# Product-key queries of a two-layer kernel: 16 column groups for both token blocks in split fp32r, against one block of 128 tokens at a time in fp32

## The chip, the cores and the metric

The kernel runs on one core of a Trainium2 chip. The metric is the device time of one execution in microseconds (us). The kernel before took 1683.35 us (median of three runs, 1680.67 to 1683.51).

## The reference

Two transformer layers on 256 tokens of width 1024. The part that changes is the first layer's feed-forward, a product-key mixture of 16384 experts, cut here to what matters:

```python
def peer_ffn(h, w_query, sub_keys, expert_u, expert_v):     # h: 256 x 1024, in two blocks of 128 tokens
    def block(xt):
        q = (xt @ w_query).reshape(128, 8, 2, 128)           # w_query: 1024 x 2048
        s = jnp.einsum('thpd,hpnd->thpn', q, sub_keys)       # 128 scores for each of 8 heads x 2 halves
        s_top, i_top = lax.top_k(s, 16)
        cand = ...                                           # 16 x 16 sums of the two halves
        best, pos = lax.top_k(cand, 16)
        idx, g = ..., jax.nn.softmax(best, axis=-1)          # 16 experts for each token and head
        act = jax.nn.gelu(jnp.einsum('td,thkd->thk', xt, expert_u[idx]))
        return jnp.einsum('thk,thkd->td', g * act, expert_v[idx])
```

Every token so gathers 128 expert rows of 8 KB (u and v side by side, `uv`). The second layer needs a vector `mod2` from its own matrix `w_ada_2`, which depends on no token.

## The kernel before

The program is one stream of instructions for each engine, laid out by a scheduler from the order and the priorities of the Python code; each engine then runs its own stream in order and waits on semaphores. SP's stream issues all plain loads, POOL's stream the gathers.

Most of the on-chip memory is one tile, `arena`, of eight slots of 2 MB (a slot is four units of 1024 columns). Slots 0 to 3 take weights in turn; slots 4 to 7 hold, in this part of the program, scratch for queries (`qT`), keys, scores (`S`) and the top-16 lists.

`_peer_scores` (line 638) makes the queries and scores. `_modulate` writes the normed tokens as two halves, `hh` and `hl` in fp32r (hi and lo, features on partitions), and the weight is split in the same way (`_halves`, line 258: ACT rounds, line 262; DVE subtracts, line 263). A product is then three fp32r matmuls, lines 274 to 276, with the weight stationary and all 256 tokens moving. There are 16 groups of 128 query columns, four to a load of `w_query` (line 716, into slots 0, 3, 1, 2); line 738 makes the scores of a load's four groups for both token blocks, against the keys. `todo[tb]` collects generators of DVE work: `top16` (lines 697 to 712) for each load and block, later `route` (lines 772 to 798), which turns the lists into `idx` (experts of a token block, transposed by PE at line 790) and `gT`. `fill(budget, blocks)` emits some of it: 2 us of block 0's after each weight group, all that is left of block 0 in one go in `_peer_experts`, and block 1's in portions of 4.5 us inside the expert loop.

`_peer_experts` first transposes the tokens to rows for the experts (`by_tokens`, line 812: `ht`, hi and lo) and forms `mod2`'s first two thirds: eight loads of `w_ada_2` (2 MB each, line 823) go through slots 0, 3, 1, 2 twice, each consumed by eight small fp32 matmuls (line 207; 32 for a set of four loads). Then comes the expert loop, over two blocks of 32 rounds r of four tokens each. For each token POOL issues a gather of 128 rows, 1 MB (line 840), into a ring of ten buffers: units 0, 2 (slot 0), 4, 6 (slot 1), 30, 22, 24 of the arena and three `uv` tiles. PE spreads the token over partitions (line 857), DVE multiplies and sums (line 859), and after four tokens PE adds the weighted v rows to `acc` (line 866), which frees the four buffers.

After the loop `_front2` and `_moe` compute the second layer.

Of the kernel before, what the change touches and what calls it, by code (L numbers as in the profile page):

```python
# [9 lines left out]
F32 = mybir.dt.float32  # L10
F32R = mybir.dt.float32r
# [3 lines left out]
AF = mybir.ActivationFunctionType  # L15
ALU = mybir.AluOpType
# [3 lines left out]
P = 128  # L20
T = 256
D = 1024
# [15 lines left out]
def _layout(i):  # L38
# [32 lines left out]
    def tiled(w, n):  # L71
        k, m = w.shape
        return w.reshape(k // P, P, m // n, n).transpose(2, 1, 0, 3).reshape(m // n, P, (k // P) * n)
# [9 lines left out]
    a["w_o_attn"] = tiled(f["w_o_attn"][0], 1024)[0]  # L83
    a["w_o_lru"] = tiled(f["w_o_lru"][0], 512)
    a["w_out"] = tiled(f["w_out"][0], 512)
    a["w_query"] = tiled(f["w_query"][0], P).reshape(4, 4, P, D).transpose(0, 2, 1, 3).reshape(4, P, 4 * D)
    a["keysT"] = f["sub_keys"][0].reshape(16, P, P).transpose(2, 0, 1).reshape(P, 16 * P)
    a["uv"] = np.concatenate([f["expert_u"][0], f["expert_v"][0]], axis=1)
    a["w_in_2"] = tiled(f["w_in_2"][0], 512)
# [149 lines left out]
def _modulate(nc, k, gain, mod, s_shift, s_scale, sq, tmp, hi, lo, y=None):  # L239

    A = tmp[:, 3 * T:3 * T + NC]
    nc.vector.scalar_tensor_tensor(A, mod[:, 8 * s_scale:8 * s_scale + 8], 1.0, gain, ALU.add, ALU.mult)
    if y is None:
        y = _stats(nc, k, sq, tmp)
    for c in range(NC):
        sh = mod[:, 8 * s_shift + c:8 * s_shift + c + 1]
        nc.vector.scalar_tensor_tensor(sq[:, c, :], k.xT[:, c, :], A[:, c:c + 1], y, ALU.mult, ALU.mult)
        nc.scalar.activation(hi[:, c, :], sq[:, c, :], AF.Identity, bias=sh)
        nc.vector.scalar_tensor_tensor(lo[:, c, :], sq[:, c, :], sh, hi[:, c, :].bitcast(F32), ALU.add, ALU.subtract)
# [386 lines left out]
def _peer_scores(tc, nc, ap, k, stage):  # L636

    ps = k.ps
    k.pe = stage.enter_context(tc.tile_pool(name="pe1", bufs=1, side="right"))
    off = [0]  # L640

    def scratch(shape, dt=F32):
        n = int(np.prod(shape))
        v = k.arena[:, 64 * T + off[0]:64 * T + off[0] + n]
        off[0] += n
        assert off[0] <= 64 * T
        if dt != F32:
            v = v.bitcast(dt)
        if len(shape) == 2:
            v = v.rearrange("p (a b) -> p a b", b=shape[1])  # L650
        if len(shape) == 3:
            v = v.rearrange("p (a b c) -> p a b c", b=shape[1], c=shape[2])
        return v

    k.scratch, k.off = scratch, off
    hh, hl = k.hr[:, :8, :], k.hr[:, 8:, :]
    off[0] = 4 * T
    _modulate(nc, k, k.col("norm2_g"), k.mod, 3, 4, scratch([NC, T]), k.arena[:, 64 * T:68 * T], hi=hh, lo=hl)

    def lin(raw, out):  # L660

        _cols3(tc, nc, k.wide, raw.rearrange("p (c n) -> p c n", c=NC), hh, hl, [out])
        k.fill(2.0, (0,))

    k.todo = todo = [[], []]

    def fill(budget, blocks=(0, 1)):

        for tb in blocks:
            while todo[tb] and budget > 0:  # L670
                got = next(todo[tb][0], None)
                if got is None:
                    todo[tb].pop(0)
                else:
                    tc.keep_in_program_order(got[0])
                    budget -= got[1]

    k.fill = fill


    off[0] = 4 * D
    qT = scratch([16, T])
    keys = scratch([16, P])
    k.S = S = [scratch([16, P]) for _ in range(2)]
    nc.sync.dma_start(keys.rearrange("p a n -> p (a n)"), ap["keysT"])
    k.best1 = best1 = []
    for tb in range(2):
        off[0] = tb * 3 * D
        best1.append((scratch([8, 2, 16]), scratch([8, 2, 16], U32), [scratch([T]) for _ in range(2)],
                      scratch([8, 16]), scratch([8, 16], U32), off[0]))  # L690

    def top16(tb, p):

        sc, (m, ix, s2, best, pos, _) = S[tb], best1[tb]
        for n in range(4 * p, 4 * p + 4):
            mv, iv, rest = m[:, n // 2, n % 2, :], ix[:, n // 2, n % 2, :], s2[n % 2][:, :P]
            yield nc.vector.max(mv[:, :8], sc[:, n, :]), 0.3
            yield nc.vector.max_index(iv[:, :8], mv[:, :8], sc[:, n, :]), 0.3
            yield nc.vector.match_replace(rest, mv[:, :8], sc[:, n, :], -3.0e38), 0.3
            yield nc.vector.max(mv[:, 8:], rest), 0.3  # L700
            yield nc.vector.max_index(iv[:, 8:], mv[:, 8:], rest), 0.3
        hs = slice(2 * p, 2 * p + 2)
        cand = sc[:, 4 * p:4 * p + 4, :].rearrange("p n k -> p (n k)").rearrange("p (h a b) -> p h a b", a=16, b=16)
        yield nc.vector.tensor_tensor(cand, m[:, hs, 0, :, None].to_broadcast([P, 2, 16, 16]),
                                      m[:, hs, 1, None, :].to_broadcast([P, 2, 16, 16]), ALU.add), 0.7
        for h in (2 * p, 2 * p + 1):
            ch, c2 = cand[:, h - 2 * p].rearrange("p a b -> p (a b)"), s2[h % 2]
            yield nc.vector.max(best[:, h, :8], ch), 0.43
            yield nc.vector.max_index(pos[:, h, :8], best[:, h, :8], ch), 0.45
            yield nc.vector.match_replace(c2, best[:, h, :8], ch, -3.0e38), 0.43  # L710
            yield nc.vector.max(best[:, h, 8:], c2), 0.43
            yield nc.vector.max_index(pos[:, h, 8:], best[:, h, 8:], c2), 0.45

    for p, sl in enumerate((0, 3, 1, 2)):
        raw = k.slot(sl)
        nc.sync.dma_start(raw, ap["w_query"][p])
        bq = [ps.tile([P, 512], F32, name="ps", tag="ps") for _ in range(2)]
        for q in range(2):
            b = bq[q]
            if p + q == 0:  # L720

                w = [_halves(tc, nc, k.wide, raw[:, u * D:(u + 1) * D].rearrange("p (c n) -> p c n", c=NC)) for u in range(3)]
                for c in range(NC):
                    for u, (wh, wl) in enumerate(w):
                        o = bq[u // 2][:, u % 2 * T:(u % 2 + 1) * T]
                        nc.tensor.matmul(o, wh[:, c], hh[:, c, :], start=c == 0 and u != 1, stop=False)
                        nc.tensor.matmul(o, wh[:, c], hl[:, c, :], start=False, stop=False)
                        nc.tensor.matmul(o, wl[:, c], hh[:, c, :], start=False, stop=c == NC - 1 and u != 0)
            for j in range(2):
                u = 2 * q + j  # L730
                if p or u == 3:
                    lin(raw[:, u * D:(u + 1) * D], b[:, j * T:(j + 1) * T])
            nc.scalar.copy(qT[:, 4 * p + 2 * q:4 * p + 2 * q + 2, :].rearrange("p a t -> p (a t)"), b)
        for tb in range(2):
            b = ps.tile([P, 512], F32, name="ps", tag="ps")
            for j in range(4):
                n = 4 * p + j
                nc.tensor.matmul(b[:, j * P:(j + 1) * P], qT[:, n, tb * P:(tb + 1) * P], keys[:, n, :],
                                 start=True, stop=True)
            nc.scalar.copy(S[tb][:, 4 * p:4 * p + 4, :].rearrange("p a n -> p (a n)"), b)  # L740
            todo[tb].append(top16(tb, p))


GU = 3
# [2 lines left out]
def _peer_experts(tc, nc, ap, k):  # L747

    with (
# [3 lines left out]
        tc.tile_pool(name="psum_a", bufs=2, space=PSUM) as k.pa,  # L753
    ):
        one, scratch, off, todo, S, best1 = k.pe, k.scratch, k.off, k.todo, k.S, k.best1
        hr = k.hr
        identr = one.tile([P, P], F32R, name="identr")
        nc.vector.tensor_copy(identr, k.ident)
        iota16 = one.tile([P, 16], F16, name="iota16")
# [44 lines left out]
        ht = one.tile([P, 2, 2, D], F32R, name="ht")  # L804

        def by_tokens(tb):
            for a in range(2):
                for g in range(2):
                    b = k.pa.tile([P, 512], F32, name="pa", tag="pa")
                    for j in range(4):  # L810
                        src = hr[:, 8 * a + 4 * g + j, tb * P:(tb + 1) * P].bitcast(F32)
                        nc.tensor.transpose(b[:, j * P:(j + 1) * P], src, k.ident)  # L812
                    nc.scalar.copy(ht[:, tb, a, 512 * g:512 * g + 512], b)


        k.csr2 = _silu_cols(nc, k, k.persist2, "c_2", "csr2")
# [6 lines left out]
                nc.sync.dma_start(ahead[g], ap[name][g])  # L823
            return ahead[g]

        by_tokens(0)
        sums = [pb.tile([P, D], F32, name="bc", tag="bc")[:, :512] for _ in range(2)]
        _ada_load(nc, load, k.csr2, sums[0], 0, range(4), "w_ada_2")
        k.fill(1e9, (0,))
        by_tokens(1)  # L830
        _ada_set(nc, k, one, sums[0], 0, k.mod2, "b_ada_2")
        _ada_load(nc, load, k.csr2, sums[1], 1, range(4), "w_ada_2")
# [54 lines left out]
def _front2(tc, nc, ap, k):  # L887
# [8 lines left out]
    with (  # L896
# [8 lines left out]
        room = k.extra.tile([P, 4 * D], F32, name="room", tag="ring")  # L905
        causal = room[:, 3584:3712]
        nc.sync.dma_start(causal, ap["masks"][:, P:2 * P])
        hh, hl = k.hr[:, :8, :], k.hr[:, 8:, :]
        sy = k.slot(1).rearrange("p (j t) -> p j t", t=T)
        big = k.slot(2).rearrange("p (j t) -> p j t", t=T)  # L910
# [444 lines left out]
```

## Time and profile before

| what | us |
|---|---|
| median of three runs | 1683.35 |
| the profiled execution | 1682.16 |
| its span, first to last instruction | 1680.3 |
| first gather issued | 348.94 |
| last gather landed | 1012.73 |

The page lists 1301.6 us of PE busy time (77% of the span), 855.5 us of DVE (51%), 308.9 us of ACT (18%). The page's slices are 42 us long: the program's first layer up to the scores lies in slices 1 to 7, the queries and the top-16 in slices 7 to 9, the expert loop in slices 9 to 25. The trace gives times from the first instruction on. A fp32 matmul shows as two records of PE, a fp32r matmul as one. Records of PE overlap, so the pitch is the distance of starts. In rows of the timeline `x3` means three instructions merged, and what stands in brackets at the end is idle time before the row and who ended it.

### The profile page before, as it was taken

The page shows a single profiled execution, that of the slowest core. Times are in us where ns is not written, and L with a number is a line of the kernel's source. Part 1 is how long each engine was busy: PE and PEld are TensorE (multiplying, and loading weights), DVE is VectorE, ACT ScalarE, POOL GpSimd, SP SyncE. Part 2 cuts the span into 40 slices and gives each one's busy share as a digit, 9 for nine tenths or more (in the row PEclk, how much of TensorE's full clock was granted, in tenths as well). Part 3 has the DMA queues.
Part 4 walks back from the last instruction along what each step waited for, and adds up shares of the span by engine and source line. Part 5 has one row for each costly group of instructions (what it writes and reads, how often), then busy time and mean ns, then how long its engine had stood idle before and what let it go on. Part 6 is the DMA issues. An engine that isn't in the chain of part 4 may idle for free.

```text
span 1680.3 us, 19564 instructions
## 1 busy us (share of the span) xinstructions
PE 1301.6 (77%) x7782; PEld 777.2 (46%) x7782; DVE 855.5 (51%) x1844; ACT 308.9 (18%) x545; POOL 242.1 (14%) x260
## 2 busy tenths in 40 slices
PE   5999999957776777777776777999978665665665
PEld 2878898623333333333333335899943221221211
DVE  4779677968884454554555446874442120121111
ACT  3567544210000000100000004443220000000000
POOL 0000000033333343333333320000000000000000
PEclk8999999978889998898889988999989888897888
DMA  9557762699999999999999997564579999999997
GB/s 377 209 224 277 278 249 101 238 371 419 420 421 420 420 420 420 415 420 420 420 420 420 420 410 277 185 250 151 225 312 429 425 427 427 427 426 429 425 429 298
DMA packets 64992, 594.56 MB, mean 354 GB/s; under 512 B 7008, under 2 KB 8064, under 8 KB 12672
## 3 DMA queue, kind: packets, MB, share of 16 engines
q1 hardware_dynamic: 28032, 324.80, 47.5%
q0 software_dynamic: 36864, 268.45, 38.6%
q8 instruction: 63, 1.03, 0.3%
q14 instruction: 33, 0.27, 0.0%
HBM read 592.15 MB, written 1.08 MB: 353 GB/s over the span
## 4 chain that ended last, share of the span: by engine, by line
DMA 43%; PE 37%; DVE 13%; issue 3%; ACT 2%; POOL 1%; SPq 0%; DVEq 0%; POOLq 0%; ACTq 0%
DMA arena<-w 19%; DMA arena<-uv,idx 12%; DMA uv<-uv,idx 9%; PE bc L857 4%; PE ps L274 4%; PE ps L276 4%; PE ps L275 4%; PE acc L866 4%; DVE arena L859 4%; DMA ring<-w 2%; PE ps L1208 2%; DVE uv L859 2%; PE ps L993 2%; PE pa L1141 1%; DVE wl L263 1%
## 5 line engine op out<-in xcount | busy, mean ns | idle before, releaser
L857 PE MATMUL bc<-ht,identr 128*128 128x512 f32 x1024 | 334.8, 455 | 172.9 <-DVE arena L859 114.6
L857 PEld LDWEIGHTS bc<-ht,identr 128*128 128x128 f32 x1024 | 191.1, 207 | 346.5 <-DVE arena L859 168.0
L859 DVE SCALAR_TENSOR_TENSOR arena<-arena,bc 128x1024 f32<-128x1024 f32 x181 | 219.9, 1219 | 170.0 <-PE bc L857 88.4
L840 POOL DMA_INDIRECT arena<-uv,idx x181 | 171.0, 945 | 660.8 <-PE pa L812 348.5
L274 PE MATMUL ps<-hr,wh 128*128 128x256 f32 x648 | 185.7, 287 | 0.0
L275 PE MATMUL ps<-hr,wh 128*128 128x256 f32 x648 | 184.5, 285 | 0.0
L276 PE MATMUL ps<-hr,wl 128*128 128x256 f32 x648 | 184.1, 284 | 0.4 <-DVE wl L263 0.4
L263 DVE TENSOR_TENSOR wl<-arena,wh 128x1024 fp32r<-128x1024 f32 (+1 forms) x116 | 139.6, 1214 | 80.1 <-ACT wh L262 79.6
L1208 PE MATMUL ps<-arena,xg 128*32 128x512 f32 x832 | 116.3, 688 | 56.1 <-DMA arena<-w 56.1
L866 PE MATMUL acc<-arena,wz 128*32 128x512 f32 x724 | 153.5, 736 | 6.5 <-DVE wz L862 6.5
L262 ACT CAST wh<-arena 128x1024 fp32r<-128x1024 f32 (+1 forms) x116 | 119.4, 1041 | 138.6 <-PE ps L275 98.7
L859 DVE SCALAR_TENSOR_TENSOR uv<-uv,bc 128x1024 f32<-128x1024 f32 x75 | 91.2, 1220 | 77.0 <-PE bc L857 45.0
L274 PEld LDWEIGHTS ps<-hr,wh 128*128 128x128 f32 x648 | 124.1, 192 | 5.1 <-issue 2.8
L860 ACT ACTIVATE s<-s 128x4 f32<-128x4 f32 x64 | 13.1, 205 | 615.1 <-DVE arena L859 366.4
L276 PEld LDWEIGHTS ps<-hr,wl 128*128 128x128 f32 x648 | 124.1, 192 | 1.4 <-DVE wl L263 1.1
L275 PEld LDWEIGHTS ps<-hr,wh 128*128 128x128 f32 x648 | 124.1, 192 | 0.9 <-issue 0.8
L1218 DVE TENSOR_TENSOR hid<-hid,ps 128x512 f32<-128x512 f32 x8 | 5.5, 688 | 209.1 <-PE ps L1208 209.1
L1231 PE MATMUL ps<-arena,hidT 128*32 128x512 f32 x400 | 65.5, 765 | 39.0 <-DMA arena<-w 36.0
L866 PE MATMUL acc<-uv,wz 128*32 128x512 f32 x300 | 90.8, 711 | 0.6 <-DVE wz L862 0.5
L1208 PEld LDWEIGHTS ps<-arena,xg 128*32 128x32 f32 x832 | 24.6, 117 | 130.1 <-DMA arena<-w 66.1
L840 POOL DMA_INDIRECT uv<-uv,idx x75 | 70.9, 945 | 87.8 <-PE acc L866 66.7
L866 PEld LDWEIGHTS acc<-arena,wz 128*32 128x32 f32 x724 | 29.1, 127 | 74.7 <-issue 44.8
(360 smaller groups left out, 1535.8 us busy)
## 6 DMA issues: line engine op xcount, KB each, us to landing
arena<-w SPq DMA_DIRECT2D x74, 2048.0 KB, 39.2
arena<-w_ada SPq DMA_DIRECT2D x24, 2048.0 KB, 10.5
arena<-w_in SPq DMA_DIRECT2D x18, 2048.0 KB, 9.0
ring<-w SPq DMA_DIRECT2D x18, 2048.0 KB, 39.2
arena<-w_query SPq DMA_DIRECT2D x4, 2048.0 KB, 11.1
arena<-w SPq DMA_DIRECT2D x6, 1024.0 KB, 15.3
arena<-w_o_lru SPq DMA_DIRECT2D x2, 2048.0 KB, 10.5
arena<-w_out SPq DMA_DIRECT2D x2, 2048.0 KB, 9.4
```

Source lines behind the costliest of these rows:

```text
L262: nc.scalar.copy(hi, w)
L263: nc.vector.tensor_tensor(lo, w, hi.bitcast(F32), ALU.subtract)
L274: nc.tensor.matmul(out, wh[:, c, cs], rh[:, c, :], start=c == 0, stop=False)
L275: nc.tensor.matmul(out, wh[:, c, cs], rl[:, c, :], start=False, stop=False)
L276: nc.tensor.matmul(out, wl[:, c, cs], rh[:, c, :], start=False, stop=c == kc - 1)
L840: nc.gpsimd.indirect_dma_start(out=uv, out_offset=None, in_=ap["uv"], in_offset=bass.IndirectOffsetOnAxis(ap=idx[:, t:t + 1], axis=0))
L857: nc.tensor.matmul(b[:, 512 * h:512 * h + 512], pick, ht[:, tb, a, 512 * h:512 * h + 512], start=a == 0, stop=a == 1)
L859: nc.vector.scalar_tensor_tensor(u, u, 1.0, b, ALU.mult, ALU.mult, accum_out=s4[:, j:j + 1])
L866: nc.tensor.matmul(acc[32 * j:32 * j + 32, 512 * h:512 * h + 512], w[:, j, 31 - r:63 - r], vs[j][:, 512 * h:512 * h + 512], start=r == 0, ...
L993: nc.tensor.matmul(b[:, j * T:(j + 1) * T], w[:, c, (2 * q + j) * P:(2 * q + j + 1) * P], src[:, c, :], start=c == 0, stop=c == 3)
L1208: nc.tensor.matmul(b[32 * j:32 * j + 32, :], xg[:, c, 32 * j:32 * j + 32], w[:, cc, j, :], start=c == 0, stop=c == NC - 1)
L1231: nc.tensor.matmul(y[h][32 * j:32 * j + 32, :], hidT[:, f, 32 * j:32 * j + 32], w[:, j], start=f == 0, stop=f == 3)
```

## The change

The queries are computed in fp32 without any split, one block of 128 tokens at a time. The 128 tokens are stationary (`hF`, features on partitions), and a load of `w_query`, now 512 columns of all 1024 rows, is moving. The queries come out with tokens on partitions, so that PE transposes them (line 740) ahead of the scores (line 746). Block 0's four loads are done first, then block 1's with the same four loads, which stay in their slots until then. `hF` takes the place of `hr`. `by_tokens` now makes the hi and lo halves itself, from `hF`, and its first call stands behind the rest of block 0's routing.

```diff
-    a["w_query"] = tiled(f["w_query"][0], P).reshape(4, 4, P, D).transpose(0, 2, 1, 3).reshape(4, P, 4 * D)
+    a["w_query"] = tiled(f["w_query"][0], 512)
...
-    hh, hl = k.hr[:, :8, :], k.hr[:, 8:, :]
+    k.hF = hF = k.persist.tile([P, NC, T], F32, name="hF", tag="hr")
...
+    for tb in range(2):
+        ts = slice(tb * P, (tb + 1) * P)
+        for c in range(NC):
+            nc.vector.scalar_tensor_tensor(sq[:, c, ts], k.xT[:, c, ts], A[:, c:c + 1], y[:, ts], ALU.mult, ALU.mult)
+            nc.scalar.activation(hF[:, c, ts], sq[:, c, ts], AF.Identity, bias=k.mod[:, 24 + c:25 + c])
...
+    raws = []
     for p, sl in enumerate((0, 3, 1, 2)):
...
+        nc.sync.dma_start(k.slot(sl), ap["w_query"][p])
+        raws.append(k.slot(sl).rearrange("p (c n) -> p c n", c=NC))
+    room = [k.arena[:, 30 * D + 512 * n:30 * D + 512 * n + 512] for n in range(4)]
...
+    def scores(tb, p):
+
+        ts = slice(tb * P, (tb + 1) * P)
+        b = bank()
+        for c in range(NC):
+            nc.tensor.matmul(b, hF[:, c, ts], raws[p][:, c, :], start=c == 0, stop=c == NC - 1)
+            if c == 3:
+                yield
+        q = room[p]
+        nc.scalar.copy(q, b)
+        yield
+        b = k.pa.tile([P, 512], F32, name="pa", tag="pa")
+        for j in range(4):
+            nc.tensor.transpose(b[:, j * P:(j + 1) * P], q[:, j * P:(j + 1) * P], k.ident)
+        nc.scalar.copy(qT[:, 4 * p:4 * p + 4, ts], b.rearrange("p (j t) -> p j t", j=4))
+        yield
+        b = bank()
+        for j in range(4):
+            n = 4 * p + j
+            nc.tensor.matmul(b[:, j * P:(j + 1) * P], qT[:, n, ts], keys[:, n, :], start=True, stop=True)
+        nc.scalar.copy(S[tb][:, 4 * p:4 * p + 4, :].rearrange("p a n -> p (a n)"), b)
+        todo[tb].append(top16(tb, p))
+        fill(1e9, (0,))
+
+    for tb in range(2):
+
+        steps = [scores(tb, p) for p in range(4)]
+        next(steps[0])
+        next(steps[0])
+        for p in range(4):
+            for _ in range(2):
+                if p < 3:
+                    next(steps[p + 1])
+                next(steps[p], None)
...
+                hi, lo = (ht[:, tb, a, 512 * g:512 * g + 512] for a in range(2))
+                nc.scalar.copy(hi, b)
+                nc.vector.tensor_tensor(lo, b, hi.bitcast(F32), ALU.subtract)
...
-        by_tokens(0)
         sums = [pb.tile([P, D], F32, name="bc", tag="bc")[:, :512] for _ in range(2)]
         _ada_load(nc, load, k.csr2, sums[0], 0, range(4), "w_ada_2")
         k.fill(1e9, (0,))
+        by_tokens(0)
         by_tokens(1)
```

What stands in the streams now, at three places.

PE, from the last scores of the queries to the first expert tokens, before (738 scores, 812 token transposes, 207 the matmuls on `w_ada_2`, 790 the transpose of block 0's indices, 857 an expert token):

```order
L738 MATMUL ps<-arena 128x128 x8
L812 MATMUL pa<-consts,hr 128x128 x8
L207 MATMUL bc<-arena,csr_2987 32x512 x40
L857 MATMUL bc<-ht,identr 128x512 x4
L207 MATMUL bc<-arena,csr_2987 32x512 x8
L790 MATMUL pa<-consts,arena 128x128
```

The same place of the change (732 queries, 740 their transposes, 746 scores, 808 the transpose of block 0's indices, 875 an expert token; block 1's last load and scores stand at the top):

```order
L732 MATMUL ps<-arena,hF 128x512 x4
L746 MATMUL ps<-arena 128x128 x4
L740 MATMUL pa<-consts,arena 128x128 x4
L746 MATMUL ps<-arena 128x128 x4
L808 MATMUL pa<-consts,arena 128x128
L828 MATMUL pa<-consts,hF 128x128 x2
L207 MATMUL bc<-arena,csr_2708 32x512 x32
L815 MATMUL pa<-consts,arena 128x128
```

Before, 48 of the 64 matmuls on `w_ada_2` stand ahead of the index transpose; now all 64 stand behind it, and it stands behind all of block 1's queries.

SP, the eight loads of `w_ada_2` and the load behind them, before, with the semaphores that each waits for:

```order
L823 DMA arena<-w_ada 128x4096 [waits DMAHW2_49,DVE_49]
L823 DMA arena<-w_ada 128x4096 [waits DMAHW5_49,DMAHW1_49,DVE_49]
L823 DMA arena<-w_ada 128x4096 [waits DVE_49]
L823 DMA arena<-w_ada 128x4096 [waits DMAHW7_49,DMAHW3_49,DVE_49]
L823 DMA arena<-w_ada 128x4096 [waits DMAHW4_49,DMAHW0_49,PE_49]
...
L178 DMA arena<-w_in 128x4096 [waits DMAHW5_49,PE_49]
```

The same of the change:

```order
L841 DMA arena<-w_ada 128x4096 [waits DMAHW2_49,PE_49]
L841 DMA arena<-w_ada 128x4096 [waits DMAHW5_49,DMAHW1_49,PE_49]
L841 DMA arena<-w_ada 128x4096 [waits PE_49]
L841 DMA arena<-w_ada 128x4096 [waits DMAHW7_49,DMAHW3_49,PE_49]
L841 DMA arena<-w_ada 128x4096 [waits DMAHW4_49,DMAHW0_49,PE_49]
...
L178 DMA arena<-w_in 128x4096 [waits DMAHW5_49,PE_49]
```

The order of the loads is the same. The first four waited for DVE's last split of the query weights in that slot, and now wait for PE's last query matmul of block 1 on it.

POOL, the first gathers, before:

```order
L840 DMA arena<-uv,idx 128x2048 x7
L840 DMA uv<-uv,idx 128x2048 x3
L840 DMA arena<-uv,idx 128x2048 x7
```

and of the change:

```order
L858 DMA arena<-uv,idx 128x2048 x3
L858 DMA uv<-uv,idx 128x2048
L858 DMA arena<-uv,idx 128x2048 x2
L858 DMA uv<-uv,idx 128x2048 x2
L858 DMA arena<-uv,idx 128x2048 x9
```

The first three are now those into units 30, 22 and 24, with the first `uv` tile behind them (tokens 4 to 7); those into slot 0 (tokens 0 and 1) come fifth and sixth, those into slot 1 (tokens 2 and 3) ninth and tenth.

## Rows read from the trace of the kernel before

**Rows 1.** The page's slices of 42 us: DMA share and GB/s.

```profile
DMA  9557762699999999999999997564579999999997
GB/s 377 209 224 277 278 249 101 238 371 419 420 421 420 420 420 420 415 420 420 420 420 420 420 410 277 185 250 151 225 312 429 425 427 427 427 426 429 425 429 298
```

**Rows 2.** Stretches: busy time of each engine, granted clock, DMA share, GB/s.

```profile
core 0: us, PE busy (x) PEld busy (x) DVE busy (x) ACT busy (x) POOL busy (x), PEclk, DMA share, GB/s
256.00:268.00 12.00, 8.59 (x60) 7.77 (x59) 9.90 (x23) 4.76 (x11) 0.00 (x0) 1.00 0.01 1
268.00:349.00 81.00, 66.06 (x526) 54.43 (x526) 70.89 (x229) 24.76 (x35) 0.06 (x1) 0.92 0.60 234
349.00:362.00 13.00, 12.27 (x65) 5.62 (x63) 3.79 (x10) 5.40 (x8) 8.20 (x9) 0.85 0.87 309
362.00:500.00 138.00, 102.33 (x421) 50.77 (x422) 119.72 (x339) 5.55 (x16) 50.48 (x53) 0.84 1.01 421
500.00:1000.00 500.00, 366.56 (x1599) 166.39 (x1597) 251.60 (x452) 14.15 (x54) 183.19 (x196) 0.90 1.01 420
```

**Rows 3.** Timeline of SP, 268 to 345 us: the loads' issues.

```profile
273.16 53.37 SPq L823 DMA_DIRECT2D arena<-w_ada  x8
335.87 0.33 SPq L178 DMA_DIRECT2D arena<-w_in  x1
```

**Rows 4.** Timeline of POOL, from 340 us: the first gathers.

```profile
348.94 1.07 POOL L840 DMA_INDIRECT arena<-uv,idx  x1 [348.48 <-PE pa L812]
350.31 0.93 POOL L840 DMA_INDIRECT arena<-uv,idx  x1 [0.30 <-issue]
353.92 0.94 POOL L840 DMA_INDIRECT arena<-uv,idx  x1 [2.67 <-PE bc L207]
```

**Rows 5.** Timeline of DVE: one task of top16 without a gap, and the route of block 0.

```profile
278.95 0.30 DVE L697 MAX8 arena<-arena 128x8 f32<-128x128 f32 x1 [0.65 <-ACT arena L740]
...
321.61 0.28 DVE L697 MAX8 arena<-arena 128x8 f32<-128x128 f32 x1
...
333.08 0.27 DVE L772 CAST arena<-arena 128x256 f16<-128x256 uint32 x1
333.27 0.22 DVE L780 TENSOR_SCALAR arena<-arena 128x128 uint32<-128x128 uint32 x1
...
346.89 0.29 DVE L789 SCALAR_TENSOR_TENSOR arena<-arena 128x128 f32<-128x128 f32 x1
```

**Rows 6.** Groups of instructions between 256 and 349 us.

```profile
L274 PE MATMUL ps<-hr,wh 128*128 128x256 f32 x104 | 30.0, 288 | 0.0
L263 DVE TENSOR_TENSOR wl<-arena,wh 128x1024 fp32r<-128x1024 f32 x14 | 16.8, 1213 | 5.7 <-ACT wh L262 5.7
L740 ACT COPY arena<-ps 128x512 f32<-128x512 f32 x8 | 4.3, 590 | 3.2 <-PE ps L738 3.2
```

**Rows 7.** Chain of waits: fp32 matmuls with 256 columns moving (64 records).

```profile
195.54 13.82 PE ps L608 x64
```

**Rows 8.** Timeline of PE: the first query, the last scores, then the `w_ada_2` matmuls.

```profile
262.26 0.50 PE L726 MATMUL ps<-hr,wh 128*128 128x256 f32 x2 [3.42 <-ACT hr L248]
...
316.26 2.00 PE L738 MATMUL ps<-arena 128*128 128x128 f32 x16
318.10 1.04 PE L812 MATMUL pa<-consts,hr 128*128 128x128 f32 x8
319.06 7.07 PE L207 MATMUL bc<-arena,csr 128*32 128x512 f32 x64
329.00 3.55 PE L207 MATMUL bc<-arena,csr 128*32 128x512 f32 x16 [2.86 <-DMA arena<-w_ada]
```

**Rows 9.** The tile `w_ada`, 250 to 400 us: its eight loads, and issue to landing.

```profile
L823 SPq DMA_DIRECT2D arena<-w_ada x8: 327/328/332, 273.2 to 326.2; - x8
DMA to landing us min/median/max: 7.8/8.3/18.4
```

**Rows 10.** POOL's waits, 340 to 1020 us: total, times, longest (us).

```profile
POOL arena L840 <- PE acc L866: 262.3, 49, 7.9
```

More of the change, by code (lines that the diff above doesn't have):

```diff
@@ L655, in _peer_scores @@
     k.scratch, k.off = scratch, off
-    hh, hl = k.hr[:, :8, :], k.hr[:, 8:, :]
+    k.hF = hF = k.persist.tile([P, NC, T], F32, name="hF", tag="hr")
     off[0] = 4 * T
[L658 to L663, printed above, removed]
+    sq, tmp = scratch([NC, T]), k.arena[:, 64 * T:68 * T]
+    A = tmp[:, 3 * T:3 * T + NC]
+    nc.vector.scalar_tensor_tensor(A, k.mod[:, 32:40], 1.0, k.col("norm2_g"), ALU.add, ALU.mult)
+    y = _stats(nc, k, sq, tmp)
+    for tb in range(2):
[3 more added lines that the diff above has]
+            nc.scalar.activation(hF[:, c, ts], sq[:, c, ts], AF.Identity, bias=k.mod[:, 24 + c:25 + c])
     k.todo = todo = [[], []]
@@ L712, in top16 @@
             yield nc.vector.max_index(pos[:, h, 8:], best[:, h, 8:], c2), 0.45
+    raws = []
     for p, sl in enumerate((0, 3, 1, 2)):
[L715 to L741, printed above, removed]
+        nc.sync.dma_start(k.slot(sl), ap["w_query"][p])
@@ new lines, in _peer_scores, with bank @@
+        raws.append(k.slot(sl).rearrange("p (c n) -> p c n", c=NC))
+    room = [k.arena[:, 30 * D + 512 * n:30 * D + 512 * n + 512] for n in range(4)]
+    def bank():
+        return ps.tile([P, 512], F32, name="ps", tag="ps")
+    def scores(tb, p):
[20 more added lines that the diff above has]
+        fill(1e9, (0,))
@@ L755, in _peer_experts @@
         one, scratch, off, todo, S, best1 = k.pe, k.scratch, k.off, k.todo, k.S, k.best1
-        hr = k.hr
         identr = one.tile([P, P], F32R, name="identr")
@@ L806, in by_tokens @@
         def by_tokens(tb):
[L807 to L813, printed above, removed]
+            for g in range(2):
+                b = k.pa.tile([P, 512], F32, name="pa", tag="pa")
+                for j in range(4):
+                    nc.tensor.transpose(b[:, j * P:(j + 1) * P], k.hF[:, 4 * g + j, tb * P:(tb + 1) * P], k.ident)
+                hi, lo = (ht[:, tb, a, 512 * g:512 * g + 512] for a in range(2))
+                nc.scalar.copy(hi, b)
+                nc.vector.tensor_tensor(lo, b, hi.bitcast(F32), ALU.subtract)
         k.csr2 = _silu_cols(nc, k, k.persist2, "c_2", "csr2")
@@ L907, in _front2 @@
         nc.sync.dma_start(causal, ap["masks"][:, P:2 * P])
+        k.hr = k.persist.tile([P, 16, T], F32R, name="hr2", tag="hr")
         hh, hl = k.hr[:, :8, :], k.hr[:, 8:, :]
```

## The prediction

> **What bounds the kernel now.** I read the page's slices first. From slice 10 to slice 23 the DMA engines move about 420 GB/s without a break; slices 7 and 8, in which the queries are made, run at 101 and 238 GB/s [rows 1]. The stretches say it sharper: from 362 to 500 us and from 500 to 1000 us the DMA share is 1.01 at 421 and 420 GB/s, while DVE is busy 119.72 of 138 us and then 251.60 of 500, and PE 102.33 and 366.56 [rows 2]. So the expert loop is bound by bytes, 256 gathers of 1.049 MB. POOL does wait 262.3 us for buffers to come free [rows 10], but with ten buffers in the ring the DMA engines have work queued all the while.
>
> Before the loop it is another matter. What ends last there is DVE: top16 starts at 278.95, the route at 333.27, its last step starts at 346.89, and the first gather is issued at 348.94 [rows 4, 5]. Beside that chain the DMA engines have room: 234 GB/s on the mean from 268 to 349 us [rows 2]. In that room lie the eight loads of `w_ada_2`, issued from 273.16 on, and one of `w_in_2` at 335.87 [rows 3]: nine of 2.097 MB, 18.9 MB, and 81 us at 234 GB/s are 19.0 MB. All nine are through when the gathers begin. Two things therefore count: when the first gather is issued, and how many bytes of loads are left to move by then, since each MB that is left costs 1 / 0.421 = 2.4 us of the loop.
>
> **The change, part by part.**
>
> *DVE loses the splits.* The subtractions of line 263 take 1.21 us each, 14 of them from 256 to 349 us [rows 6]. Nine fall between the first top16 step and the route, so the top16 of block 0 spans 54.1 us (278.95 to 333.08). One task without a split takes 321.61 to 333.08, 11.47 us [rows 5]; four are 45.9 us, 8.2 less. `lo` for the experts adds four subtractions of half the size behind the route, some 2.4 us by the same row; they end ahead of the first gather's landing, and I cost them at nothing.
>
> *PE: the first scores come no sooner.* A fp32 matmul is two records; with 256 columns a record takes 13.82 / 64 = 0.216 us [rows 7], so with 512 columns the eight matmuls of a load take 16 x 0.432 = 6.9 us. Four score matmuls take half of 2.00 us, four transposes the 1.04 us of line 812 [rows 8]. The queries start as now, at 262.2 [rows 8]: fewer columns per step shorten what each waits for by tenths. By the new stream the first scores follow the first load (6.9), two halves of the second (3.5 each), transposes and scores (1.0 each): 278.1, and ACT's copy of 0.59 [rows 6] makes it 278.7, as today. Later scores come every 8.9 us, faster than DVE's 11.5. So top16 ends at 278.7 + 45.9 = 324.6.
>
> *The route* takes 333.27 to 347.18, 13.9 us [rows 5]: its last step ends at 338.5. From there to the first gather took 1.76 us (347.18 to 348.94), now 340.3: **8.6 us sooner**. PE must be done with block 1 by 338.5, because the transpose of the indices stands behind it. A block is 4 x 8.9 us and about 1 us of waiting at its end: block 0 ends at 298.9, block 1 at 335.6. It fits by 3 us.
>
> *What the query weights now hold up.* Slot 0 comes free for its `w_ada_2` load only when block 1 has used it, at 298.9 + 6.9 = 305.8; the next three follow at 8.9 us each, the fourth at some 331.5 to 332.5, and with 7.8 to 8.3 us from issue to landing [rows 9] it is there at 340. The second four wait for PE's 32 matmuls on the first four, which stand behind the index transpose: they start at 339 and need 7.07 us, or twice that at half clock, as 16 records did in 3.55 us after a pause [rows 8]. The fifth load is thus issued at 341 to 343, the eighth at 347 to 353. So at the first gather four of the eight loads and the one of `w_in_2` have not started: 5 x 2.097 = 10.5 MB, at the loop's 0.421 MB per us, **24.9 us** that lay in an idle stretch and now lie in the loop. A bound from below is four loads, 19.9 us, if the `w_in_2` load finds a gap; from above five and a part of the fourth, 27 us.
>
> That sum takes it that loads and gathers share one capacity. Loads alone ran at 425 to 429 GB/s in the slices of the experts of the second layer, gathers alone at 420 [rows 1]; no row shows both at full rate. The Trainium skill, "DMA: Bandwidth & Descriptors", section "Issuing engines are not separate DMA queues", says that DMAs of SP, ACT and POOL run on the same 16 engines and interleave whoever started them. By that rule the 24.9 us stand in full; without it the sum would keep only the 8.6 us gained. The share of 1.01 with one queue busy agrees with the rule as far as a trace with one busy queue can.
>
> *A new wait in the ring.* POOL issues four gathers into free buffers, then waits for slot 0 until PE has used the fifth load, and for slot 1 until it has used the seventh; tokens 8 and 9 have buffers but stand behind on POOL. No buffer is freed until tokens 0 to 3 are all through. Queued work meanwhile: four gathers 10 us, four loads 20, `w_in_2` 5, tokens 0, 1, 8, 9 10, tokens 2 and 3 5: 50 us, to about 393. The seventh load is there by 375, tokens 2 and 3 by 385 to 392, and product, gelu and `acc` add some 5 us before POOL can issue again: a gap of 0 to 8 us. DVE then has 13% slack (119.72 of 138 us), so it may hold a round or two up. The first gathers today lose something too: 309 GB/s over 13 us are 4.0 MB [rows 2], 3.5 us short of full rate from 348.94, of which up to 1 us returns because the queue is now full from the start. I take +3 net, between 0 and +10.
>
> *At nothing:* the normed tokens (same columns in 16 steps for 8, lo gone), ACT's extra query copies (0.59 us each on an engine busy 24.76 of 81 us [rows 2]), the tail of the loop and the second layer, which begin when the last gather lands.
>
> **Sum:** -8.6 + 24.9 + 3 = +19.3 us on the profiled 1682.16: 1701.5. That execution lies 1.2 us below the median of 1683.35, within the runs shown; I say **1701 us**. 0.2% (3.4 us) is about what a measurement of this kernel can tell from no change.
>
> **The rivals.**
>
> 1. *The loads ride beside the gathers* and the shorter chain stays: 1682.2 - 8.6 = 1673.6, faster. It decides if the engines can take more than 421 GB/s when two queues are full, which for 10.5 MB over the 40 us in question would be 680 GB/s. For it: slices 31 on show a little more with loads. Against: the share of 1.01. Chance 0.05.
>
> 2. *Much of it is given back*: the deferred bytes cost only what the loop cannot absorb, should POOL's waits of 262.3 us be real slack after all. Then the 24.9 shrink to between 5 and 12 and the time is 1679 to 1689. Against: 420 GB/s in each slice of the loop. Chance 0.08, most of it within 0.2% or slower.
>
> 3. *Block 1 is late for the index transpose.* If fp32 matmuls with a stationary block run 10% slower than line 608's, block 1 ends at 343 and everything moves by 4 us; at half clock from 320 on, by 15: 1705 to 1716. For it: fp32 weight loads of 128 columns for each 512. Against: the granted clock was 1.00 to 0.92 here [rows 2]. Chance 0.1.
>
> 4. *The ring stalls for longer*, because in-order POOL and PE hold one another up over the first rounds: +10 to +20 in place of +3, 1709 to 1719. Chance 0.09.
>
> **How the numbers follow.** The forecast, 1692 to 1709, has 0.68: low with 19.9 for the loads and no gap (1682.2 - 8.6 + 19.9 = 1693.5, less 1 for a prompt start), high with a gap of 10. The range for 8 in 10 takes in the lower halves of rivals 3 and 4: 1691 to 1712. Faster by over 0.2%: rival 1 and a part of rival 2, 0.06; within 0.2%: 0.04; slower: 0.90.
>
> **What would show it.** Right: first gather issued at 339 to 342; the first `w_ada_2` load issued at 305 to 307 and the fifth after 340; GB/s from 256 to 340 halved, then 420 from about 343; the last gather landed some 19 us later than 1012.73. Wrong: a first gather after 345 (rival 3), stretches above 430 GB/s near 350 (rival 1), DMA share below 0.9 between 385 and 420 (rival 4), or a loop that ends before 1015.

## The result, and the profile after

The changed kernel takes 1711.03 us (median of four runs, 1709.58 to 1712.16), the kernel before 1683.13: ratio 1.0173, 95% interval 1.0161 to 1.0186. It is slower by 28 us; the forecast of 1701 us made it 18. The profiled execution took 1709.58 us, 27.4 more than that of before.

The stretches of [rows 2], cut finer, first one of the kernel before, then those of the changed kernel (us, then busy time of each engine, granted clock, DMA share, GB/s):

```profile
268.00:340.00 72.00, 64.29 (x520) 53.32 (x519) 63.46 (x218) 24.35 (x34) 0.00 (x0) 0.97 0.57 220
```

```profile
268.00:340.00 72.00, 62.30 (x220) 33.09 (x222) 57.44 (x216) 15.26 (x26) 0.06 (x1) 0.96 0.32 117
340.00:349.00 9.00, 9.00 (x67) 2.29 (x59) 0.78 (x3) 0.27 (x2) 3.83 (x4) 0.78 0.83 309
349.00:362.00 13.00, 8.59 (x37) 3.17 (x36) 3.23 (x6) 2.76 (x5) 0.94 (x1) 0.74 1.00 423
362.00:385.00 23.00, 7.68 (x36) 3.28 (x38) 2.46 (x4) 0.00 (x0) 2.81 (x3) 0.63 1.01 424
385.00:420.00 35.00, 25.47 (x134) 11.54 (x127) 24.68 (x80) 2.48 (x5) 13.19 (x14) 0.94 0.69 269
420.00:500.00 80.00, 62.17 (x251) 29.05 (x250) 71.79 (x221) 1.65 (x8) 27.88 (x30) 0.81 1.01 420
500.00:1000.00 500.00, 380.44 (x1588) 171.50 (x1589) 261.89 (x471) 16.81 (x56) 187.16 (x200) 0.86 1.01 420
```

From 268 to 340 us the DMA engines move 117 GB/s where it was 220. From 349 to 385 they are full, loads and gathers together. From 385 to 420 the share falls to 0.69, which is new, and from 420 on the loop runs as before, at 420 GB/s.

The timeline of POOL, which answers to [rows 4], and the last gather:

```profile
339.94 1.08 POOL L858 DMA_INDIRECT arena<-uv,idx  x1 [339.48 <-DVE arena L810]
...
343.81 0.94 POOL L858 DMA_INDIRECT uv<-uv,idx  x1 [0.30 <-issue]
360.76 0.94 POOL L858 DMA_INDIRECT arena<-uv,idx  x1 [16.02 <-PE bc L207]
...
386.35 0.94 POOL L858 DMA_INDIRECT arena<-uv,idx  x1 [20.92 <-PE bc L207]
388.03 0.94 POOL L858 DMA_INDIRECT arena<-uv,idx  x1 [0.74 <-PE bc L207]
402.50 0.94 POOL L858 DMA_INDIRECT arena<-uv,idx  x1 [13.54 <-PE acc L884]
...
1015.80 0.94 POOL L858 DMA_INDIRECT arena<-uv,idx  x1 [0.30 <-issue]
```

The first gather is 9.0 us sooner than the 348.94 of before. Then POOL stands still three times: 16 us for slot 0 (tokens 0 and 1), 21 us for slot 1 (tokens 2 and 3), 13.5 us until the first round of four tokens is added up and returns its buffers. The last gather is issued 25.8 us later than before (990.01).

SP's timeline answers to [rows 3]; the first row covers all eight loads of `w_ada_2`, the second the last four of them:

```profile
303.62 45.57 SPq L841 DMA_DIRECT2D arena<-w_ada  x8
343.32 5.87 SPq L841 DMA_DIRECT2D arena<-w_ada  x4
365.63 0.33 SPq L178 DMA_DIRECT2D arena<-w_in  x1
```

PE's timeline shows why slot 1 came so late (line 207: the matmuls on `w_ada_2`; 875: a token's broadcast; 884: the sum of a round):

```profile
363.65 1.92 PE L207 MATMUL bc<-arena,csr 128*32 128x512 f32 x16 [0.89 <-DMA arena<-w_ada]
374.67 2.07 PE L875 MATMUL bc<-ht,identr 128*128 128x512 f32 x4 [9.10 <-DVE arena L877]
382.08 2.07 PE L875 MATMUL bc<-ht,identr 128*128 128x512 f32 x4 [5.33 <-DVE arena L877]
384.08 5.70 PE L207 MATMUL bc<-arena,csr 128*32 128x512 f32 x32
...
400.33 1.92 PE L884 MATMUL acc<-arena,wz 128*32 128x512 f32 x16
```

The matmuls on the seventh and eighth load stand behind the broadcasts of tokens 1 and 2. These wait for DVE's product of the token before, and so for gathers that had themselves waited for slot 0.

### The profile page after: what moved, and what is told of

Its sections match the earlier page's. It is cut to its first block, busy times and chain, and to the rows that moved or that the text cites. A ratio compares the mean times of both kernels' runs of the same rounds, so it can differ in the third digit from the quotient of the medians.

```text
span 1707.8 us, 19046 instructions
## 1 busy us (share of the span) xinstructions
PE 1334.2 (78%) x7542; PEld 757.4 (44%) x7542; DVE 837.5 (49%) x1832; ACT 297.1 (17%) x541; POOL 241.7 (14%) x260
## 3 DMA queue, kind: packets, MB, share of 16 engines
q1 hardware_dynamic: 28032, 324.80, 46.7%
## 4 chain that ended last, share of the span: by engine, by line
DMA 44%; PE 36%; DVE 13%; issue 4%; ACT 2%; POOL 1%; SPq 0%; DVEq 0%; POOLq 0%; ACTq 0%
DMA arena<-w 18%; DMA arena<-uv,idx 17%; PE acc L884 4%; DVE arena L877 4%; PE ps L274 4%; PE ps L276 4%; PE ps L275 4%; PE bc L875 3%; DMA uv<-uv,idx 3%; DMA ring<-w 2%; PE ps L1227 2%; PE ps L1012 2%; DMA arena<-w_ada 1%; PE pa L1160 1%; DVE uv L877 1%
## 5 line engine op out<-in xcount | busy, mean ns | idle before, releaser
L875 PE MATMUL bc<-ht,identr 128*128 128x512 f32 x1024 | 340.2, 460 | 169.1 <-DVE arena L877 120.5
L884 PE MATMUL acc<-arena,wz 128*32 128x512 f32 x724 | 163.6, 779 | 6.3 <-DVE wz L880 6.3
L274 PE MATMUL ps<-hr,wh 128*128 128x256 f32 x544 | 155.7, 286 | 0.0
L275 PE MATMUL ps<-hr,wh 128*128 128x256 f32 x544 | 155.1, 285 | 0.0
L263 DVE TENSOR_TENSOR wl<-arena,wh 128x1024 fp32r<-128x1024 f32 (+1 forms) x100 | 120.4, 1214 | 70.6 <-ACT wh L262 70.2
L276 PE MATMUL ps<-hr,wl 128*128 128x256 f32 x544 | 154.6, 285 | 0.0
L262 ACT CAST wh<-arena 128x1024 fp32r<-128x1024 f32 (+1 forms) x100 | 102.8, 1040 | 111.8 <-PE ps L275 80.9
L274 PEld LDWEIGHTS ps<-hr,wh 128*128 128x128 f32 x544 | 104.2, 191 | 4.8 <-issue 2.8
L275 PEld LDWEIGHTS ps<-hr,wh 128*128 128x128 f32 x544 | 104.2, 192 | 0.9 <-issue 0.8
L276 PEld LDWEIGHTS ps<-hr,wl 128*128 128x128 f32 x544 | 104.2, 192 | 0.7 <-DVE wl L263 0.4
L884 PE MATMUL acc<-uv,wz 128*32 128x512 f32 x300 | 95.7, 755 | 1.1 <-DVE wz L880 1.1
## 6 DMA issues: line engine op xcount, KB each, us to landing
arena<-w_ada SPq DMA_DIRECT2D x24, 2048.0 KB, 10.6
```

The lines of the kernel that those rows point to most:

```text
L262: nc.scalar.copy(hi, w)
L263: nc.vector.tensor_tensor(lo, w, hi.bitcast(F32), ALU.subtract)
L274: nc.tensor.matmul(out, wh[:, c, cs], rh[:, c, :], start=c == 0, stop=False)
L275: nc.tensor.matmul(out, wh[:, c, cs], rl[:, c, :], start=False, stop=False)
L276: nc.tensor.matmul(out, wl[:, c, cs], rh[:, c, :], start=False, stop=c == kc - 1)
L875: nc.tensor.matmul(b[:, 512 * h:512 * h + 512], pick, ht[:, tb, a, 512 * h:512 * h + 512], start=a == 0, stop=a == 1)
```

## The experiments

In all of them the rest of the kernel is as changed, if not said otherwise. `keep_in_program_order` pins an instruction behind all that is already written on its engine. Each was timed against the kernel before on its own chip (1681.2 to 1681.5 us there).

**1. PE's order alone.**

```diff
-    nc.tensor.matmul(b[:, 512 * h:512 * h + 512], pick, ...)
+    mm = nc.tensor.matmul(b[:, 512 * h:512 * h + 512], pick, ...)
+    if t + h + a == 0:
+        tc.keep_in_program_order(mm)
```

> The changed kernel, with PE's 32 matmuls on the second four loads of w_ada_2 all ahead of the first token's broadcast; nothing else moves. Theory A: the time beyond the forecast (1711 against 1701) is the ring. In the changed kernel slots 0 and 1 of the ring come free only when PE has used the fifth to the seventh load, and on PE the seventh and eighth stand behind the broadcasts of tokens 1 and 2, which wait for DVE's product of the token before and so for gathers that were themselves held up. Then slot 1 comes free at 370 to 376 instead of 386, the DMA gap at 392 to 404 shrinks to 4 us at most, and the time is 1699 to 1704. Theory B: the gap is not made by this order but by the bytes alone, or the time beyond the forecast lies in the steady loop (granted clock 0.86 instead of 0.90): 1708 to 1713.

Measured: 1709.36 us, ratio 1.0148 (1.0126 to 1.0170), in theory B's range. POOL's timeline and the last stretch of this kernel:

```profile
375.44 0.94 POOL L858 DMA_INDIRECT arena<-uv,idx  x1 [7.21 <-PE bc L207]
377.15 0.94 POOL L858 DMA_INDIRECT arena<-uv,idx  x1 [0.77 <-PE bc L207]
403.70 0.94 POOL L858 DMA_INDIRECT arena<-uv,idx  x1 [25.62 <-PE acc L886]
```

```profile
385.00:420.00 35.00, 25.79 (x110) 13.33 (x108) 25.10 (x77) 1.79 (x4) 8.31 (x9) 0.80 0.69 277
```

Slot 1 came free at 375 as theory A had it, and no gain can be told from noise: by the medians both kernels are 27.9 us above the kernel before, and the intervals of the two ratios overlap. Tokens 2 and 3 are still the last of ten gathers in the queue, so the first round closes only when the queue is empty. Theory A was incomplete.

**2. The index transpose behind the matmuls on the first four loads**, as before the change.

```diff
-            nc.tensor.transpose(b[:, :P], sel[0]..., k.ident)
+            tc.keep_in_program_order(nc.tensor.transpose(b[:, :P], sel[0]..., k.ident))
```

> The changed kernel, with the transpose of block 0's indices pinned behind PE's 32 matmuls on the first four loads of w_ada_2, as it stood before the change. Theory A (bytes left at the first gather, and the ring): these matmuls then run from 330 to 339, as soon as block 1's queries are done, the fifth to seventh load are issued at 332 to 337 instead of 341 to 347, some 6 us of bytes move into the idle stretch and the ring's gap mostly closes: 1691 to 1701, first gather at 340 to 341. Rival: PE's wait for the fourth load (landing at 337 to 340) delays the transpose and so the first gather by as much as it saves: 1705 to 1711, first gather after 343.

Measured: 1697.75 us, ratio 1.0093 (1.0072 to 1.0115), in theory A's range; the first gather came at 339.75, a little ahead of its 340 to 341. From 385 to 420 us the share is 0.83, so that the gap is closed in part. The fifth load is issued at 333.21 instead of 343.32, and some 12 us of the 28 are back by the order of 33 instructions on PE.

**3 and 4. No loads of `w_ada_2`**, in the changed kernel and in the one before.

```diff
-                nc.sync.dma_start(ahead[g], ap[name][g])
```

> The changed kernel without its eight loads of w_ada_2; the matmuls run on what lies in the slots, so that mod2 is made from query weights. Theory A: four loads less to move in the loop (19.9 us at 0.421 MB per us) and no ring gap (some 10 us): 1677 to 1683, last gather issued near 986 to 990, and the steady loop runs as in the changed kernel. Theory B (the rest lies in the steady loop or the tail): 1688 to 1692.

> The kernel before without its eight loads of w_ada_2, mod2 made from query weights. If the loads rode free in the idle stretch before the first gather, as the forecast took it: 1679 to 1684, at most the 3.5 us of the slow start of the gathers are gained. If they cost the loop something even there: below 1677.

Measured: 1690.40 us, ratio 1.0042 (1.0026 to 1.0059), and 1682.74 us, ratio 1.0003 (0.9988 to 1.0017). In the kernel before the eight loads are free, as expected. In the changed one they cost some 19 us by the medians (27.9 less 9.0), about what four loads take at 0.421 MB per us, 19.9. But without them it is still 7 us (by the ratio) to 9 us (by the medians) slower than the kernel before, in spite of the earlier indices: the 64 matmuls keep their place behind the index transpose, slots 0 and 1 wait for them, and the ring starts late (a DMA share of 0.43, 0.75 and 0.83 in the three stretches from 340 to 385 us). Theory A was wrong on the third run. The time lies in theory B's range, though not for theory B's reason: the steady loop runs at 419 to 421 GB/s. The third run's stretches from 340 to 385 us:

```profile
340.00:349.00 9.00, 6.79 (x43) 2.09 (x47) 3.27 (x8) 0.31 (x1) 2.95 (x3) 0.63 0.43 146
349.00:362.00 13.00, 13.00 (x101) 4.25 (x97) 3.23 (x6) 2.83 (x5) 2.25 (x3) 1.00 0.75 272
362.00:385.00 23.00, 15.94 (x71) 8.80 (x67) 11.10 (x28) 2.28 (x4) 4.32 (x5) 0.78 0.83 338
```

**5. POOL's order alone**, and **6. both orders**.

```diff
-            nc.gpsimd.indirect_dma_start(out=uv, ...)
+            tc.keep_in_program_order(nc.gpsimd.indirect_dma_start(out=uv, ...))
```

> The changed kernel with POOL's gathers held to the order of the tokens, so that nothing is gathered before slot 0 is free. Theory A (order of the ring): in the changed kernel and in the first experiment tokens 4 to 9 are gathered ahead of 2 and 3, so that the first round is the last of the queue to land and no buffer comes free before the queue is empty. In order, the first gather is issued 21 us later, at 360 to 362, while the loads alone keep the DMA engines busy to about 368; the gap moves to 373 to 382, where tokens 2 and 3 wait for PE's seventh matmul group, and no second gap follows: 1703 to 1709 in spite of the late start. Theory B (the gap is only the time from landing to release and does not depend on the order; gathers issued first are a gain): 1715 to 1725.

> The changed kernel with both edits: gathers in the order of the tokens, and PE's matmuls on the second four loads ahead of the first broadcast. Theory A: slots 0 and 1 come free by 370, before the loads' bytes are through, so that the DMA engines never run dry, and only the bytes are left of the loss: 1697 to 1703, DMA share 0.95 or more in each stretch from 345 to 420. Theory B: 1709 or more, as with either edit alone.

Measured: 1710.42 us, ratio 1.0174 (1.0160 to 1.0188), and 1701.12 us, ratio 1.0116 (1.0095 to 1.0137). The stretches, first of the fifth, then of the sixth:

```profile
362.00:385.00 23.00, 9.11 (x40) 3.48 (x40) 3.61 (x6) 1.87 (x2) 4.93 (x6) 0.63 0.70 281
385.00:420.00 35.00, 27.51 (x107) 14.07 (x108) 28.73 (x96) 0.62 (x3) 13.81 (x15) 0.80 1.01 414
```

```profile
340.00:349.00 9.00, 8.03 (x51) 2.39 (x55) 2.06 (x7) 0.31 (x1) 0.00 (x0) 0.65 0.27 87
349.00:362.00 13.00, 9.85 (x71) 3.31 (x63) 3.24 (x6) 2.83 (x5) 2.02 (x2) 1.00 1.01 429
362.00:385.00 23.00, 13.70 (x57) 5.53 (x57) 4.91 (x9) 1.92 (x3) 7.50 (x8) 0.70 1.00 421
385.00:420.00 35.00, 26.97 (x115) 11.88 (x115) 29.61 (x107) 0.77 (x4) 11.26 (x12) 0.80 1.01 412
```

In order alone, the gap only moves ahead, to where tokens 2 and 3 wait for PE (their gather is issued at 378.42); the gain was nil, below what theory A gave. With both edits the gap from 385 to 420 is gone and 8 to 10 us come back, though the first gather is issued 17 us later than in the changed kernel (357.28) and the engines stand idle at the start instead (a share of 0.27 from 340 to 349). Either order alone is enough to hold the ring; that is why the first and the fifth run showed no gain.

**7. The first four loads' matmuls between block 1's queries**, with the edits of 2, 5 and 6. Their sum has a PSUM bank of its own, and those on the fifth and sixth load stand ahead of the index transpose.

```diff
+            if tb and p:
+                ada(p - 1)
+    ada(3)
...
-        _ada_load(nc, load, k.csr2, sums[0], 0, range(4), "w_ada_2")
+        _ada_load(nc, load, k.csr2, sums[1], 1, range(2), "w_ada_2")
```

> The changed kernel with gathers in order, the matmuls on the first four loads of w_ada_2 set between block 1's queries, so that their slots are loaded again before the first gather, and those on the fifth and sixth load ahead of the index transpose. Bytes left at the first gather: two to three loads in place of five. Theory A: 9 to 15 us less than the fifth or sixth experiment's bytes and no gap: 1681 to 1688, first gather at 340 to 343. Rival: waits for landings between block 1's queries hold PE and with it the index transpose: first gather at 345 to 350 and 1686 to 1695.

Measured: 1686.58 us, ratio 1.0027 (1.0016 to 1.0038). From 349 us on the share is 1.00 to 1.01. The time lies in both ranges, which overlap from 1686 to 1688, and so decides nothing; the first gather, at 348.72, is the rival's, because PE waits for the landing of the sixth load ahead of the index transpose:

```profile
344.28 3.46 PE L207 MATMUL bc<-arena,csr 128*32 128x512 f32 x16 [4.04 <-DMA arena<-w_ada]
347.68 0.43 PE L837 MATMUL pa<-consts,arena 128*128 128x128 f32 x1
```

It cost little, since the loads used the time.

**8 to 10. A buffer of their own for four, then five loads.**

```diff
-            ahead[g] = k.slot(next(ring))
+            ahead[g] = pre if g < 4 else k.slot(next(ring))
...
+            if (tb, p) in ((0, 1), (0, 3), (1, 0), (1, 2)):
+                ada(2 * tb + p // 2)
+                if 2 * tb + p // 2 < 3:
+                    load("w_ada_2", 2 * tb + p // 2 + 1)
```

> As the seventh, but the first four loads of w_ada_2 go one after the other through a 2 MB buffer of their own (the room of the splits' halves, which the changed kernel no longer uses there), the first of them ahead of all queries, and their matmuls stand between the queries of both blocks; the second four go into slots 0, 3, 1, 2 as block 1 releases them. At the first gather only a part of the eighth load and the load of w_in_2 are left, 2.5 to 3.5 MB, 6 to 8 us. Theory A (bytes left and ring order are all that the change costs, and the 8.6 us of DVE are a real gain): 1675 to 1681, below the kernel before. Theory B (something else costs as well, or the gain of DVE does not reach the end): 1683 to 1690.

> As the eighth, but five loads of w_ada_2 go through the buffer of their own, each used a step earlier, the other three into slots 0, 1 and 2, so that slot 3 takes the load of w_in_2 as soon as block 1 has used it; the fifth's partial sum is added by one matmul with the identity. Theory A: at 340 at most 1 MB of loads is left (4.1 MB in the eighth), first gather at 341 to 343: 5 to 7 us less than the eighth run, 1673 to 1677, below the kernel before by 0.2 to 0.5%. Theory B (the eighth run's remaining distance is not bytes): 1679 to 1682.

> As the ninth, with the index transpose ahead of PE's matmuls on the sixth load. Theory A: the indices are there 1 to 2 us sooner, but the first gather goes into slot 0, which waits for those matmuls, so that nothing is gained: within 1.5 us of the ninth run, 1673 to 1678. Rival (the index transpose decides): 2 us less than the ninth.

Measured: 1680.36 us, ratio 0.9994 (0.9985 to 1.0003); 1679.24, ratio 0.9985 (0.9976 to 0.9994); 1678.27, ratio 0.9982 (0.9973 to 0.9992). The eighth undoes the loss, as its theory A had it. The tenth takes 1.9% less than the changed kernel (0.9982 against 1.0173) and lies just below the kernel before. The ninth fell in theory B's range: its first gather came at 347.60, not 341 to 343, as its queries began at 265.12 (260.75 in the eighth) and its five groups of matmuls, and those on the sixth load, stand ahead of the index transpose. The tenth is 1.0 us below the ninth; that is within theory A's 1.5 us, but the intervals overlap and do not exclude the rival's 2. Its first gather is issued at 345.92, 3.0 us sooner than in the kernel before: of the 8.6 us of DVE, only about 3 have been turned into time.

## Where the prediction went wrong, and what of it held

The measured 1711 us lies 2 us above the forecast's upper end of 1709. The path was right: bytes pushed from an idle stretch into a loop that is bound by bytes. The step that failed is the ring, where a gap "of 0 to 8 us" and "+3 net" were taken and +11 was measured.

**One account for all runs.** In every kernel the loop is at 419 to 421 GB/s from 420 us on, so the bytes moved by then should set the end. I take the GB/s of one stretch, 250 to 420 us, times its 170 us (with 16.8 MB added where the eight loads are left out); what is missing against the kernel before, divided by 0.421, is the time to expect. The rows of the kernel before, of the changed one and of the tenth run:

```profile
250.00:420.00 170.00, 136.06 (x877) 94.36 (x876) 138.60 (x433) 38.84 (x62) 28.22 (x30) 0.90 0.70 279
```

```profile
250.00:420.00 170.00, 127.87 (x541) 63.44 (x540) 95.71 (x332) 26.48 (x54) 20.83 (x22) 0.88 0.53 211
```

```profile
250.00:420.00 170.00, 148.09 (x647) 74.62 (x646) 127.16 (x440) 28.23 (x59) 31.73 (x34) 0.94 0.72 288
```

| kernel | MB by 420 us | from bytes, us | that execution, us | measured, medians, us |
|---|---|---|---|---|
| before | 47.4 | 0 | 0 | 0 |
| changed | 35.9 | +27.5 | +27.4 | +27.9 |
| 1 PE's order | 35.2 | +29.1 | +27.2 | +27.9 |
| 2 index transpose behind | 40.8 | +15.7 | +14.3 | +16.3 |
| 3 no loads, changed | 43.0 | +10.6 | +14.2 | +9.0 |
| 4 no loads, before | 46.7 | +1.7 | +2.9 | +1.3 |
| 5 POOL's order | 37.2 | +24.2 | +25.1 | +28.9 |
| 6 both orders | 38.9 | +20.2 | +19.9 | +19.6 |
| 7 woven | 45.7 | +4.0 | +4.4 | +5.1 |
| 8 own buffer | 48.5 | -2.4 | -3.7 | -1.1 |
| 9 five loads | 48.3 | -2.0 | -1.0 | -1.9 |
| 10 index first | 49.0 | -3.6 | -4.4 | -2.9 |

The bytes are those of one profiled execution, so its own time (above the 1682.16 of before) belongs beside them: ten of eleven agree within 2 us, and the third is 3.6 off. By the medians ten of eleven agree within 2 us too, and the fifth is 4.7 off. Behind the loop little changes: from the issue of the last gather to the end of the span it is 690 to 693 us in all twelve kernels, 690.3 before and 692.0 in the changed one. So nearly the whole effect lies in that stretch.

**Point by point.**

- *DVE loses the splits*: right. Top16 ran from 278.66 to the route at 324.76, the first gather came at 339.94; forecast were 278.7, 324.6 and 340.3. To meet the last within 0.4 us was in part luck: the queries began at 260.97, not 262.2, and in the first run, which issues the same work up to there, the first gather came at 342.17.
- *PE*: right, with room to spare. A load's queries took 6.9 us; block 1 was done at 330.5 instead of 335.6, and PE stood idle 8.3 us before the index transpose. Rival 3 did not happen.
- *What the query weights hold up*: right. The first load was issued at 303.62 (forecast 305 to 307), the fifth at 343.32 (341 to 343), each a little outside. By 340 us 117 GB/s x 72 us = 8.4 MB of 18.9 had moved, so 10.5 MB were left as forecast, 24.8 us. Loads and gathers together made 423 and 424 GB/s here and 429 at most in the sixth run, no more than the loads alone (425 to 429 [rows 1]): rival 1 is out, and the 19 us between the third run and the changed kernel leave next to nothing of rival 2. The Trainium skill, "DMA: Bandwidth & Descriptors", section "Issuing engines are not separate DMA queues", says that DMAs started by different engines run on the same 16 DMA engines and interleave; these rates agree, now with both queues busy.
- *A new wait in the ring*: **here the prediction failed**, in the size of a term, "+3 net, between 0 and +10". The engines lost 9 x (1.01 - 0.83) + 35 x (1.01 - 0.69) = 12.8 us between 340 and 420; the kernel before lost 13 x (1.01 - 0.87) = 1.8 in its first 13 us [rows 2]. That is 11 net, the lower end of what rival 4 named. The failed step is the gap of "0 to 8 us": it let tokens 2 and 3 land "by 385 to 392", ahead of the end of the queued work at 393, with the seventh load used when it landed, "by 375". In fact PE reached that load at 384, behind broadcasts that wait for DVE. And this wait alone does not make the gap: tokens 2 and 3 are the last of ten gathers, so the queue is empty when they land, and the engines stand until the first round is added up and the next gather starts. The rows of the changed kernel, then one of the first run, where both gathers are issued 11 us sooner (375.44 against 386.35):

```profile
385.00:394.00 9.00, 5.42 (x35) 1.52 (x28) 1.23 (x2) 1.87 (x2) 1.87 (x2) 0.82 0.85 312
394.00:404.00 10.00, 8.41 (x43) 4.44 (x41) 7.73 (x24) 0.21 (x1) 1.19 (x2) 1.00 0.04 17
```

```profile
394.00:404.00 10.00, 8.37 (x32) 4.79 (x33) 7.71 (x21) 0.20 (x1) 0.30 (x1) 0.65 0.04 16
```

  The engines stand for the same 10 us in both. The "some 5 us" from product to issue were 6.4 in the changed kernel (396.11 to 402.50) and 7.3 in the first run (396.42 to 403.70), with nothing else queued. A part of them is DVE's order, which the prediction did not price: behind token 3's product at 396.11 DVE makes two products of the next round before it forms the weights of this one (`wz`, line 880):

```profile
396.11 1.22 DVE L877 SCALAR_TENSOR_TENSOR arena<-arena,bc 128x1024 f32<-128x1024 f32 x1 [2.80 <-DMA arena<-uv,idx]
...
399.77 0.16 DVE L880 TENSOR_TENSOR wz<-s,gT 128x4 f32<-128x4 f32 x1
```

  No run moves `wz` ahead, so what that order costs is not shown.
- *The sum*: -9.0 + 24.8 + 11.0 = +26.8, measured +27.4. The sixth run's 1701.1 us is the forecast's own figure by chance: its gap is gone, but its first gather is 17 us later, which the forecast did not have.

Of the signs named ahead, the first gather, the fifth load and the halved rate came as said; the first load came 1.4 us early, the full rate at 349 and not 343, and the last gather 25.8 us later and not 19. The share below 0.9 between 385 and 420, the sign of rival 4, came too, at 0.69. One outcome cannot tell whether its chance of 0.09 was too low; but POOL's order, with tokens 2 and 3 ninth and tenth, was known, and it says that the queue runs empty before a buffer comes free.

## What to carry to other kernels

When a loop is bound by bytes, count the bytes that have moved by the time it reaches full rate; an edit ahead of it is worth what it does to that count, and not what it saves on the engine that ends last there. Buffers that are held for longer cost the transfers that were to go into them: ask for each what idle stretch its load filled. In a ring that is filled for the first time, follow which group closes first: if its members are last in the queue, the ring runs dry once. Where two in-order streams each hold it, as here, curing one of them may show no gain until the other is cured too.

## What the runs showed that was not expected

- The sixth run differs from the first only in POOL's order. It starts the gathers 15 us later (357.28 against 342.17) and is 8 us faster (1701.12 against 1709.36).
- A longer wait was followed by half the pace on PE, just when its result was awaited. In the first run the same 16 records on a load took 1.92 us after a pause of 1.55 us, at a granted clock of 1.00 (2.4 GHz), and 3.64 after one of 5.46, at 0.50 (1.2 GHz):

```profile
365.82 1.92 PE L207 MATMUL bc<-arena,csr 128*32 128x512 f32 x16 [1.55 <-DMA arena<-w_ada]
373.20 3.64 PE L207 MATMUL bc<-arena,csr 128*32 128x512 f32 x16 [5.46 <-DMA arena<-w_ada]
```

```profile
365.50:368.00 2.50, 1.92 (x16) 0.42 (x16) 0.00 (x0) 0.00 (x0) 1.89 (x3) 1.00 1.01 429
372.50:377.00 4.50, 3.64 (x16) 0.60 (x16) 0.00 (x0) 0.00 (x0) 0.94 (x1) 0.50 1.02 430
```

- The same first part of the program began its queries at 260.75 in one execution and at 265.12 in another. No run here tells how much of the spread of some 5 us between runs of one kernel comes from there.
